# x's first mixer straight behind the first block, the context's choice beside it, and the context's gathered rows spread into layer 1

## The chip, the cores and the metric

One core of a Trainium2 chip runs the kernel. Its engines are PE (TensorE, matrix products), DVE (VectorE, element-wise work and reductions), ACT (ScalarE, activation functions and copies), POOL (GpSimd, here a queue that starts transfers) and SP (SyncE, the other queue that starts transfers). Each engine works through its own instructions in the order in which they stand. The metric is the device time of one execution in microseconds (us); a run of the kernel before takes 3798.77 us (median of three).

## The reference

Everything is float32 on 256 tokens of width 1024. A first block makes x: a banded attention layer, a latent attention layer and a norm. A second block has two layers over x and over a context of 256 tokens. Each layer makes from a conditioning vector the shifts, scales and gates that modulate both streams, runs a mixer (attention over x and context together, a pooling branch, a convolution branch, gates), and then a feed-forward with experts (PEER):

```python
xn = modulate(rms_norm(h, norm1_g[l]), mod[:, 0], mod[:, 1])
cn = modulate(rms_norm(hc, norm1_g[l]), mod_c[0], mod_c[1])
...                                   # q, k, v of x; k, v of the context
o = blocked_diff_attn(q, jnp.concatenate([k, kc], axis=1), jnp.concatenate([v, vc], axis=1), lam)
mix = mixer_output(o, p, ...)
if not last: hc = hc + mod_c[2] * mix_c          # the context's own mixer: layer 0 alone
h = h + mod[:, 2] * mix
h = h + mod[:, 5] * peer_ffn(xn2, ...)
if not last: hc = hc + mod_c[5] * peer_ffn(cn2, ...)   # the context's feed-forward: layer 0 alone
```

`peer_ffn` scores every token against two sets of 128 keys per head, takes the 16 best of each and the 16 best sums (the choice), and so picks 8 x 16 of 16384 experts per token. An expert is a row of `peer_u` (a dot product with the token, then gelu) and a row of `peer_v` (added with the gate as weight).

## The kernel before

Weights that are not read whole are split into a high part (ACT cast, L277, `wa`) and a rest (DVE subtraction, L278, `wb`), and a product is three matmuls (L405 to L407). For x the feed-forward is dense: `peer` walks the 16384 experts in 128 tiles of 128; `hid` makes a tile's activations, `wgt` multiplies them with a table of gates `G` that `gbuild` has written to memory (L1412), and `vside` (L1475 to L1477) adds the tile to four accumulators. For the context it is sparse: `rows` gathers 512 blocks (256 of `pu`, 256 of `pv`; block i holds the i-th chosen expert's row for each of 128 tokens, 512 KB) by an indirect transfer on POOL (L1335), and DVE makes a dot product (L1346) or a weighted addition (L1355) of each. Below, such a block is called a row.

The program is a set of Python generators. Each `yield` gives an estimate of the work just written, and combinators decide whose instructions come next: `par` advances the generator that is least far on relative to its total, `along` advances a side generator by a rate times the main one's cost, `chain` puts generators behind one another. A scheduling layer then rearranges a little within a window of some tens of instructions. So the order on each engine is fixed when the program is built.

`program` writes these stages in this order (L1569 to L1616), with the times of the profile below:

- 0 to 835 us: `b1`, the first block, beside the context's mixer of layer 0 and behind that the context's choice (`choose`, that is `topk` with `rows=True`); `mods` of layer 0 beside the context's attention.
- 835 to 1262: x's mixer of layer 0, with rows at a rate of 0.28 (`RATE[0]`).
- 1262 to 1575: `ffn_start` of layer 0: x's choice (`topk`), `gbuild`, the first tiles of `hid`, `mods` of layer 1 (48 blocks of `wmod`, 96 matmuls at L554 that the profile counts as 192), and rows at 0.28.
- 1575 to 2459: the tiles of `peer`, with rows by `par` and the total 270 (`RLEFT`); the rows that are left run on alone, and `rows_add` adds the context's sum.
- 2459 to 2911: x's mixer of layer 1; the context's norm, k and v (`kv_ctx`) beside x's q, k and v.
- 2911 to the end: `ffn_start` and `peer` of layer 1, without rows and without `mods`.

Tiles of one size share a pool of 42 buffers (`pg`).

Of the kernel before, what the change touches and what calls it, by code (L numbers as in the profile page):

```python
# [9 lines left out]
F32 = mybir.dt.float32  # L10
# [29 lines left out]
AT = 350.0  # L40
RLAG, RDEPTH = 20, 4
RATE, RLEFT = (0.28, 0.28), 270.0
# [246 lines left out]
class Ker:  # L289
# [228 lines left out]
    def mods(s, l, eng):  # L518
# [21 lines left out]
        for g in range(3):  # L540
            if g == 1 and l == 0:
                s.mod_scale(l, (("a1", "n1", 1),))
                yield None
                lim = 48
                for i in range(NMD):
                    load(16 + i)
            bank = s.ps("m")
            for q in range(16):
# [7 lines left out]
                if q % 4 == 3 and q < 15:  # L556
                    yield 2.0
# [578 lines left out]
    def mixer(s, l, st, src, ws, eng, res, kvx, late=None, before=None, seq=False, h=None, rbs=None):  # L1136
# [10 lines left out]
        qg = s.qkv(l, hn, ws, rope, True, r)  # L1147
        yield from (qg if before is None else par(s, (qg, 100.0), (before, 80.0)))
        o = Act(s, F32, "o")
        kv = [(r["k"], r["v"])] + kvx()  # L1150
        sr, q = r.pop("sr"), r.pop("q")
        if st == 1:
            for i in range(2):
                eng.dma_start(s.kvd[i], r["k"].t[i].rearrange("p k t -> p (k t)"))
                eng.dma_start(s.kvd[2 + i], r["v"][i])
        r.clear()
        more = [(late, 20.0)] if late is not None else []
        if seq:
            yield from par(s, (s.attn2(l, q, kv, sr, o), 60.0), *more)
            del q, kv, sr  # L1160
            yield from s.branches(l, hn, ws, r)
        else:
            yield from par(s, (s.attn2(l, q, kv, sr, o), 60.0), (s.branches(l, hn, ws, r), 190.0), *more)
            del q, kv, sr
# [142 lines left out]
    def rows(s, xn, out):  # L1307

        nc, v = s.nc, s.nc.vector
        xr = []  # L1310
# [226 lines left out]

def until(g):
# [18 lines left out]
def ffn_start(k, l, rx, ws, G, pe, tot, *more):  # L1557
# [5 lines left out]
    yield from par(k, (chain(tk, lambda: k.gbuild(rx, G, eng)), TG), (until(pe), tot), *more)  # L1563


def program(k, upto):
# [15 lines left out]
    def choose():  # L1582
        yield from k.topk(0, rc["xn"], wc, gp, rc, rows=True)
        cn.append(rc.pop("xn"))
    drain(par(k, (b1, 300.0),
              (chain(k.mixer(0, 1, ctx0, wc, gp, rc, lambda: [], md, seq=True, h=hc.pop(), rbs=rbc.pop()),
                     choose), AT),
              (k.setup2(), 100.0)))
    if upto < 3:
        return  # L1590
    rows = k.rows(cn, acc)
    ws = WS(k, ai["w2"][0], sy, whole=WHOLE)
    drain(along(k.mixer(0, 0, k.hd["x"], ws, sy, rx, lambda: [k.kv_load(sy)], seq=SEQ, h=x3.pop()), rows, RATE[0]))
    kp = {}
    pe = k.peer(0, rx["xn"], k.G[0], sy, sy, *NPRE[0], k.hd["x"], kp)
    drain(along(ffn_start(k, 0, rx, ws, k.G[0], pe, NPRE[0][1] * 3.41, (k.mods(1, gp), 60.0)), rows, RATE[1]))
    rx.clear()
    drain(par(k, (pe, 130 * 5.12), (rows, RLEFT)))
# [31 lines left out]
```

## Time and profile before

| | us |
|---|---|
| median of three runs (3797.86 to 3800.38) | 3798.77 |
| the profiled execution | 3794.38 |
| its span, first to last instruction | 3792.6 |
| PE busy | 3334.0 (88%) |
| DVE busy | 2739.1 (72%) |
| ACT busy | 1495.4 (39%) |
| POOL busy | 904.3 (24%) |

The profile is one execution on the chip. Busy is the time in which an engine ran an instruction; PEclk is the share of TensorE's full clock (2.4 GHz) that was granted; the DMA share is the mean busy share of the 16 transfer engines. Matmuls are pipelined, so one that lasts 0.28 us can be followed by the next after 0.12 us, and a busy PE is not at its peak. Waits are inferred from semaphores.

### The profile page before, as it was taken

The page shows a single profiled execution, that of the slowest core. Times are in us where ns is not written, and L with a number is a line of the kernel's source. Part 1 is how long each engine was busy: PE and PEld are TensorE (multiplying, and loading weights), DVE is VectorE, ACT ScalarE, POOL GpSimd, SP SyncE. Part 2 cuts the span into 40 slices and gives each one's busy share as a digit, 9 for nine tenths or more (in the row PEclk, how much of TensorE's full clock was granted, in tenths as well). Part 3 has the DMA queues.
Part 4 walks back from the last instruction along what each step waited for, and adds up shares of the span by engine and source line. Part 5 has one row for each costly group of instructions (what it writes and reads, how often), then busy time and mean ns, then how long its engine had stood idle before and what let it go on. Part 6 is the DMA issues. An engine that isn't in the chain of part 4 may idle for free.

```text
span 3792.6 us, 58009 instructions
## 1 busy us (share of the span) xinstructions
PE 3334.0 (88%) x21940; PEld 2974.1 (78%) x21940; DVE 2739.1 (72%) x5629; ACT 1495.4 (39%) x2807; POOL 904.3 (24%) x863
## 2 busy tenths in 40 slices
PE   7998999969899857789999994299999699999999
PEld 6966999857898844678888884187998588999998
DVE  4356775597898797898888899855765986555555
ACT  3444553213544122334444442142552154544444
POOL 2010011112223325655445457600000030000000
PEclk9988999978899879899999997598999899999999
DMA  8554445426678739999999999841445097666664
GB/s 295 178 182 136 133 147 186 179 84 255 217 249 312 283 138 398 403 401 372 363 370 370 371 369 361 331 156 58 154 150 200 23 289 256 216 211 210 211 210 143
DMA packets 249945, 907.32 MB, mean 239 GB/s; under 512 B 27632, under 2 KB 29712, under 8 KB 249664
## 3 DMA queue, kind: packets, MB, share of 16 engines
q1 hardware_dynamic: 126240, 454.09, 34.1%
q0 software_dynamic: 123424, 449.52, 32.6%
q8 instruction: 172, 2.82, 0.3%
q14 instruction: 109, 0.89, 0.1%
HBM read 861.53 MB, written 45.11 MB: 239 GB/s over the span
## 4 chain that ended last, share of the span: by engine, by line
PE 46%; DVE 7%; DMA 5%; issue 3%; ACT 1%; POOL 1%; DVEq 0%; ACTq 0%; POOLq 0%
PE pu L407 8%; PE pu L405 7%; PE pu L406 7%; PE pm L1475 5%; PE pm L1476 5%; PE pm L1477 5%; PE pu L412 3%; DMA row<-in_pu,ridx 2%; DMA row<-in_pv,ridx 1%; DVE wb L278 1%; DVE racc L1355 1%; PE pm L1403 1%; ACT wa L277 1%; DMA wm<-in_wmod 1%; POOL row L1335 1%
## 5 line engine op out<-in xcount | busy, mean ns | idle before, releaser
L278 DVE TENSOR_TENSOR wb<-wr,wa 128x1024 fp32r<-128x1024 f32 x846 | 1011.0, 1221 | 322.4 <-ACT wa L277 310.4
L277 ACT CAST wa<-wr 128x1024 fp32r<-128x1024 f32 x846 | 854.6, 1048 | 23.4 <-DMA wr<-in_w 17.8
L405 PE MATMUL pu<-hnh,wa 128*128 128x256 f32 x2000 | 584.4, 292 | 24.9 <-ACT wa L277 22.3
L407 PE MATMUL pu<-hnh,wb 128*128 128x256 f32 x2000 | 581.6, 291 | 8.2 <-DVE wb L278 8.2
L406 PE MATMUL pu<-hnl,wa 128*128 128x256 f32 x2000 | 580.6, 291 | 1.5 <-DVE hnl L501 1.3
L406 PE MATMUL pu<-xl,wa 128*128 128x256 f32 x1760 | 499.9, 284 | 9.2 <-DVE xl L1444 9.2
L405 PE MATMUL pu<-xh,wa 128*128 128x256 f32 x1760 | 499.7, 284 | 6.3 <-ACT xh L1443 3.9
L407 PE MATMUL pu<-xh,wb 128*128 128x256 f32 x1760 | 499.8, 284 | 0.8 <-DVE wb L278 0.8
L1335 POOL DMA_INDIRECT row<-in_pv,ridx x256 | 362.8, 1417 | 385.1 <-DVE wb L278 131.1
L1335 POOL DMA_INDIRECT row<-in_pu,ridx x256 | 332.3, 1298 | 472.4 <-PE pu L407 113.8
L405 PEld LDWEIGHTS pu<-hnh,wa 128*128 128x128 f32 x2000 | 398.3, 199 | 32.5 <-ACT wa L277 26.2
L1475 PE MATMUL pm<-wa,W 128*128 128x512 f32 x1024 | 368.2, 397 | 60.1 <-ACT wa L277 58.4
L1476 PE MATMUL pm<-wb,W 128*128 128x512 f32 x1024 | 409.8, 400 | 4.5 <-DVE wb L278 4.3
L407 PEld LDWEIGHTS pu<-hnh,wb 128*128 128x128 f32 x2000 | 397.2, 199 | 15.4 <-DVE wb L278 11.0
L1477 PE MATMUL pm<-wa,W 128*128 128x512 f32 x1024 | 404.2, 395 | 0.0
L406 PEld LDWEIGHTS pu<-hnl,wa 128*128 128x128 f32 x2000 | 398.4, 199 | 4.0 <-DVE hnl L501 2.5
L405 PEld LDWEIGHTS pu<-xh,wa 128*128 128x128 f32 x1760 | 339.1, 193 | 20.4 <-ACT wa L277 7.4
L406 PEld LDWEIGHTS pu<-xl,wa 128*128 128x128 f32 x1760 | 339.0, 193 | 16.5 <-DVE xl L1444 9.6
L407 PEld LDWEIGHTS pu<-xh,wb 128*128 128x128 f32 x1760 | 339.3, 193 | 2.3 <-DVE wb L278 1.0
L1346 DVE CUSTOM_DVE_ANT_0 row<-row,xr 128x1024 f32<-128x1024 f32 x256 | 310.9, 1219 | 28.0 <-DMA row<-in_pu,ridx 28.0
L1355 DVE SCALAR_TENSOR_TENSOR racc<-row,rwg,racc 128x1024 f32<-128x1024 f32 x254 | 325.4, 1281 | 7.5 <-DMA row<-in_pv,ridx 6.8
L412 PE MATMUL pu<-xn,wr 128*128 128x256 f32 x1344 | 320.7, 397 | 4.8 <-ACT xn L514 4.8
(403 smaller groups left out, 5408.7 us busy)
## 6 DMA issues: line engine op xcount, KB each, us to landing
wr<-in_w SPq DMA_DIRECT2D x288, 512.0 KB
wr<-in_pu SPq DMA_DIRECT2D x256, 512.0 KB
wr<-in_pv SPq DMA_DIRECT2D x256, 512.0 KB
wr<-in_w POOLq DMA_DIRECT2D x130, 512.0 KB
wm<-in_wmod POOLq DMA_DIRECT2D x96, 512.0 KB
G<-gt POOLq DMA_DIRECT2D x64, 512.0 KB
gp<-G SPq DMA_DIRECT2D x32, 512.0 KB
gp<-G POOLq DMA_DIRECT2D x32, 512.0 KB
```

The source lines that it names most:

```text
L277: nc.scalar.copy(a, r)
L278: nc.vector.tensor_tensor(b, r, a, op=OP.subtract)
L405: mm(out, ah, bh, start=i == 0, stop=False)
L406: mm(out, ah, bl, start=False, stop=False)
L407: mm(out, al, bh, start=False, stop=i == n - 1)
L412: s.nc.tensor.matmul(out, w[:, k * 128:(k + 1) * 128], x(k), start=k == 0, stop=k == 7)
L1335: nc.gpsimd.indirect_dma_start(out=t, out_offset=None, in_=tab[w], in_offset=bass.IndirectOffsetOnAxis(ap=s.ridx[:, tt, i:i + 1], axis=0))
L1346: v.tensor_tensor_reduce(t, t, xr[tt], 1.0, 0.0, OP.mult, OP.add, hid[:, i:i + 1])
L1355: v.scalar_tensor_tensor(out[tt], t, wg[:, i:i + 1], out[tt], op0=OP.mult, op1=OP.add)
L1475: mm(bank, wh, vh[:, c], start=j == 0, stop=False)
L1476: mm(bank, wh, vl[:, c], start=False, stop=False)
L1477: mm(bank, wl, vh[:, c], start=False, stop=j == 127)
```

## The change

What it does, part by part:

1. `b1` and x's mixer of layer 0 become one chain, and a new combinator `lead` follows it with side generators: the context's mixer and choice, then the rows, at twice the chain's cost (`RATE[0]` = 2.0); a row there has the cost 6.25, so rows come at 0.32 per unit. `rows` waits until the choice has been written.
2. `mods` of layer 1 moves from x's `ffn_start` of layer 0 to the context's choice, by `par` with 69 to 26. Its yields become finer. `mods` of layer 0 stands beside the context's branches, and not beside its attention.
3. Rows: 0.32 in x's mixer, 0.25 in `ffn_start`, 0.45 per unit beside the tiles of `peer` (a tile is 5.12), 0.3 beside x's q, k and v of layer 1, and the rest ahead of `rows_add` in `kv_ctx`. By the two instruction orders, rows stand in x's mixer, `ffn_start`, the tiles and behind the tiles thus: before 100, 53, 272, 87; now 113, 41, 300, 58.
4. In x's mixer of layer 1, `kv_ctx` stands no longer beside q, k and v: it is chained ahead of the attention, and that chain runs beside the branches.
5. `gbuild` starts the writes of `G` from ACT and not from POOL.

```diff
--- before.py
+++ after.py
@@ -37,9 +37,9 @@
 W1, NMD = 8, 5
 SEQ, TY = False, 1.0
 SW, ST = 40.0, 240.0
-AT = 350.0
 RLAG, RDEPTH = 20, 4
-RATE, RLEFT = (0.28, 0.28), 270.0
+RATE = 2.0, 0.32, 0.25, 0.45, 0.3, 2.0
+RLATE = 150.0
 GS = 2.0 ** 15
 DEPTH, LEAD = 3, 2
 DU, LU, DV, LV = 2, 1, 2, 1
@@ -544,6 +544,7 @@
                 lim = 48
                 for i in range(NMD):
                     load(16 + i)
+                yield 1.0
             bank = s.ps("m")
             for q in range(16):
                 kt, hf = q // 2, q % 2
@@ -553,8 +554,8 @@
                     j = hf * 2 + jj
                     nc.tensor.matmul(bank[32 * j:32 * j + 32, :], s.cs[:, kt, :],
                                      w[:, jj * 512:(jj + 1) * 512], start=kt == 0, stop=kt == 7)
-                if q % 4 == 3 and q < 15:
-                    yield 2.0
+                if q < 15:
+                    yield 0.5
             ev = s.s2([128, 512], "mev")
             nc.scalar.copy(ev, bank)
             tb = s.ps("m")
@@ -1133,7 +1134,8 @@
                 v.tensor_tensor(mrg.pair(i), mrg.pair(i), th, op=OP.add)
             yield 2.6
 
-    def mixer(s, l, st, src, ws, eng, res, kvx, late=None, before=None, seq=False, h=None, rbs=None):
+    def mixer(s, l, st, src, ws, eng, res, kvx, late=None, before=None, seq=False, h=None, rbs=None, side=None):
+
 
         nc, v = s.nc, s.nc.vector
         rope = st == 0
@@ -1144,24 +1146,33 @@
         del h, rbs
         yield 1.0
         r = {}
-        qg = s.qkv(l, hn, ws, rope, True, r)
-        yield from (qg if before is None else par(s, (qg, 100.0), (before, 80.0)))
-        o = Act(s, F32, "o")
-        kv = [(r["k"], r["v"])] + kvx()
-        sr, q = r.pop("sr"), r.pop("q")
+        yield from (s.qkv(l, hn, ws, rope, True, r) if side is None else
+                    along(s.qkv(l, hn, ws, rope, True, r), side, RATE[4]))
+        o = []
         if st == 1:
             for i in range(2):
                 eng.dma_start(s.kvd[i], r["k"].t[i].rearrange("p k t -> p (k t)"))
                 eng.dma_start(s.kvd[2 + i], r["v"][i])
+        q, sr, kv = r.pop("q"), r.pop("sr"), [(r["k"], r["v"])]
         r.clear()
+
+        def attend():
+            o.append(Act(s, F32, "o"))
+            kv.extend(kvx())
+            yield from s.attn2(l, q, kv, sr, o[0])
+            kv.clear()
         more = [(late, 20.0)] if late is not None else []
         if seq:
-            yield from par(s, (s.attn2(l, q, kv, sr, o), 60.0), *more)
-            del q, kv, sr
-            yield from s.branches(l, hn, ws, r)
+            yield from attend()
+            del q, sr
+            yield from par(s, (s.branches(l, hn, ws, r), 30.0), *more)
+        elif before is not None:
+            yield from par(s, (chain(before, attend), RLATE), (s.branches(l, hn, ws, r), 150.0), *more)
+            del q, sr
         else:
-            yield from par(s, (s.attn2(l, q, kv, sr, o), 60.0), (s.branches(l, hn, ws, r), 190.0), *more)
-            del q, kv, sr
+            yield from par(s, (attend(), 60.0), (s.branches(l, hn, ws, r), 190.0), *more)
+            del q, sr
+        o = o.pop()
         s.dump(f"o{l}{st}", o)
         mrg = r.pop("mrg")
         yield from s.gate_add(ws, hn, o, mrg)
@@ -1307,6 +1318,8 @@
     def rows(s, xn, out):
 
         nc, v = s.nc, s.nc.vector
+        while not xn:
+            yield 0.0
         xr = []
         cn = xn.pop()
         for tt in range(2):
@@ -1535,6 +1548,23 @@
         yield from g() if callable(g) else g
 
 
+def lead(main, *sides):
+
+    t, live = 0.0, [[g, r, 0.0] for g, r in sides]
+    for c in main:
+        t += c or 0.0
+        for e in live:
+            while e[2] < t * e[1]:
+                d = next(e[0], math.inf)
+                e[2] += d or 0.0
+        yield c
+
+
+def scaled(g, f):
+    for c in g:
+        yield c * f
+
+
 def until(g):
 
     for c in g:
@@ -1560,7 +1590,7 @@
     tk = k.topk(l, rx["xn"], ws, eng, rx)
     for i in range(SOLO):
         yield next(tk, None)
-    yield from par(k, (chain(tk, lambda: k.gbuild(rx, G, eng)), TG), (until(pe), tot), *more)
+    yield from par(k, (chain(tk, lambda: k.gbuild(rx, G, k.nc.scalar)), TG), (until(pe), tot), *more)
 
 
 def program(k, upto):
@@ -1582,32 +1612,31 @@
     def choose():
         yield from k.topk(0, rc["xn"], wc, gp, rc, rows=True)
         cn.append(rc.pop("xn"))
-    drain(par(k, (b1, 300.0),
-              (chain(k.mixer(0, 1, ctx0, wc, gp, rc, lambda: [], md, seq=True, h=hc.pop(), rbs=rbc.pop()),
-                     choose), AT),
-              (k.setup2(), 100.0)))
-    if upto < 3:
-        return
     rows = k.rows(cn, acc)
     ws = WS(k, ai["w2"][0], sy, whole=WHOLE)
-    drain(along(k.mixer(0, 0, k.hd["x"], ws, sy, rx, lambda: [k.kv_load(sy)], seq=SEQ, h=x3.pop()), rows, RATE[0]))
+    ctx = chain(k.mixer(0, 1, ctx0, wc, gp, rc, lambda: [], md, seq=True, h=hc.pop(), rbs=rbc.pop()),
+                lambda: par(k, (choose(), 69.0), (k.mods(1, gp), 26.0)))
+    xs = chain(b1, lambda: k.mixer(0, 0, k.hd["x"], ws, sy, rx, lambda: [k.kv_load(sy)], seq=SEQ, h=x3.pop()))
+    drain(lead(xs, (chain(ctx, lambda: scaled(rows, RATE[0] / RATE[1])), RATE[0]), (k.setup2(), 0.5)))
     kp = {}
     pe = k.peer(0, rx["xn"], k.G[0], sy, sy, *NPRE[0], k.hd["x"], kp)
-    drain(along(ffn_start(k, 0, rx, ws, k.G[0], pe, NPRE[0][1] * 3.41, (k.mods(1, gp), 60.0)), rows, RATE[1]))
+    drain(along(ffn_start(k, 0, rx, ws, k.G[0], pe, NPRE[0][1] * 3.41), rows, RATE[2]))
     rx.clear()
-    drain(par(k, (pe, 130 * 5.12), (rows, RLEFT)))
-    k.rows_add(0, acc, kp)
-    acc.clear()
+    drain(along(pe, rows, RATE[3]))
     if upto < 5:
         return
     ws = WS(k, ai["w2"][1], sy, whole=WHOLE)
     wc = WS(k, ai["w2"][1, 8:24], gp)
 
     def kv_ctx():
+        yield from scaled(rows, RATE[5])
+        k.rows_add(0, acc, kp)
+        acc.clear()
         hn = k.norm_hl(kp.pop(1), lambda i: k.a1[1][:, i, 1:2], k.mod(1, 1, 0), "hnc")
         yield 1.0
         yield from k.qkv(1, hn, wc, False, False, rc)
-    drain(k.mixer(1, 0, k.hd["x"], ws, sy, rx, lambda: [(rc.pop("k"), rc.pop("v"))], before=kv_ctx(), h=kp.pop(0)))
+    drain(k.mixer(1, 0, k.hd["x"], ws, sy, rx, lambda: [(rc.pop("k"), rc.pop("v"))], before=kv_ctx(), h=kp.pop(0),
+                  side=rows))
     pe = k.peer(1, rx["xn"], k.G[1], sy, gp, *NPRE[1], ao)
     drain(ffn_start(k, 1, rx, ws, k.G[1], pe, NPRE[1][1] * 3.41))
     rx.clear()
```

PE around the context's choice (L1207 and L412 before, L1218 and L412 now, `pm<-keyT` and `pu<-xn`). Before, the choice has PE to itself and x's norm (L471) follows:

```order
L1207 MATMUL pm_7803<-keyT_7468,qf_7801 128x128 x4
L412 MATMUL pu_7931<-xn_7393,wr_7842 128x256 x4
L412 MATMUL pu_7931<-xn_7394,wr_7842 128x256 x4
L412 MATMUL pu_7931<-xn_7393,wr_7883 128x256 x4
L412 MATMUL pu_7931<-xn_7394,wr_7883 128x256 x2
L1207 MATMUL pm_7854<-keyT_7468,qf_7852 128x128 x4
L412 MATMUL pu_7931<-xn_7394,wr_7883 128x256 x2
L1207 MATMUL pm_7903<-keyT_7468,qf_7901 128x128 x4
L1207 MATMUL pm_7950<-keyT_7468,qf_7948 128x128 x4
L471 MATMUL pm_8099<-ones,sq_8100 128x1 x8
L471 MATMUL pm_8099<-ones,sq_8110 128x1 x8
```

Now matmuls of the first block's last product (`ogh`, `ogl`) and of `mods` (L555, `wm`) stand between:

```order
L406 MATMUL pu_7774<-ogl_6464,wa_7678 128x256
L407 MATMUL pu_7774<-ogh_6462,wb_7679 128x256
L555 MATMUL pm_7570<-wm_7726,cs 32x512 x2
L1218 MATMUL pm_7648<-keyT_6918,qf_7646 128x128 x4
L412 MATMUL pu_7813<-xn_6822,wr_7636 128x256 x4
L412 MATMUL pu_7813<-xn_6823,wr_7636 128x256 x4
L412 MATMUL pu_7813<-xn_6822,wr_7716 128x256 x4
L412 MATMUL pu_7813<-xn_6823,wr_7716 128x256 x3
L1218 MATMUL pm_7746<-keyT_6918,qf_7744 128x128 x4
L412 MATMUL pu_7813<-xn_6823,wr_7716 128x256
L555 MATMUL pm_7570<-wm_7730,cs 32x512 x2
L405 MATMUL pu_7905<-ogh_6461,wa_7777 128x256
```

The choice's matmuls have moved into the first block's end, and `mods` of layer 1 with them.

POOL in `gbuild` of layer 0, before: gathers of rows (L1335), loads for `mods` (L536) and writes of `G` (L1412) in one queue:

```order
L536 DMA wm_13682<-in_wmod 128x1024
L536 DMA wm_13686<-in_wmod 128x1024
L536 DMA wm_13690<-in_wmod 128x1024
L536 DMA wm_13694<-in_wmod 128x1024
L1335 DMA row_13698<-in_pv,ridx 128x1024
L1412 DMA G_96<-gt_13477 128x8x128
L1412 DMA G_96<-gt_13478 128x8x128
L1412 DMA G_96<-gt_13479 128x8x128
```

ACT at the same place now: the writes of `G` (L1425) stand behind the evictions that fill them (`gt`), and POOL's queue there holds gathers alone:

```order
L1420 ACTIVATE gt_13483<-pm_13633 128x32x4
L1420 ACTIVATE gt_13484<-pm_13633 128x32x4
L1425 DMA G_96<-gt_13481 128x8x128
L1425 DMA G_96<-gt_13482 128x8x128
L1425 DMA G_96<-gt_13483 128x8x128
L1425 DMA G_96<-gt_13484 128x8x128
L1420 ACTIVATE gt_13653<-pm_13663 128x32x4
L1420 ACTIVATE gt_13654<-pm_13663 128x32x4
```

DVE behind the last tile of layer 0, before: rows, and between them only x's norm for layer 1 (L392, L474) at the very end:

```order
L1346 ISA row_22468,rhid<-row_22468,xr_8237 128x1024
L1346 ISA rhid 128x1
L1355 SCALAR_TENSOR_TENSOR racc_18006<-row_22471,rwg,racc_18006 128x1024
L1346 ISA row_22474,rhid<-row_22474,xr_8237 128x1024
L1346 ISA rhid 128x1
L1355 SCALAR_TENSOR_TENSOR racc_18006<-row_22477,rwg,racc_18006 128x1024
L474 TENSOR_REDUCE ss_22632<-pm_22611 128x2
L392 TENSOR_SCALAR rt_22636<-ss_22632 128x2
L1346 ISA row_22480,rhid<-row_22480,xr_8237 128x1024
```

DVE in x's q, k and v of layer 1 now: a row between every one or two weight rests (L278, `wb`):

```order
L278 TENSOR_TENSOR wb_22597<-wr_22561,wa_22596 128x1024
L1359 ISA row_22557,rhid<-row_22557,xr_8469 128x1024
L1359 ISA rhid 128x1
L278 TENSOR_TENSOR wb_22632<-wr_22594,wa_22631 128x1024
L1363 TENSOR_TENSOR rwg<-rwg,rgate 128x16
L1368 SCALAR_TENSOR_TENSOR racc_17674<-row_22591,rwg,racc_17674 128x1024
L278 TENSOR_TENSOR wb_22662<-wr_22629,wa_22661 128x1024
L1359 ISA row_22625,rhid<-row_22625,xr_8469 128x1024
L1359 ISA rhid 128x1
L278 TENSOR_TENSOR wb_22697<-wr_22659,wa_22696 128x1024
L278 TENSOR_TENSOR wb_22732<-wr_22694,wa_22731 128x1024
L1368 SCALAR_TENSOR_TENSOR racc_17674<-row_22690,rwg,racc_17674 128x1024
```

So 58 rows have moved past the start of x's mixer of layer 1, and none stands alone.

## Rows read from the trace of the kernel before

**Rows 1.** The page's slices: PE's busy share in tenths, 40 slices of 94.8 us.
```profile
PE   7998999969899857789999994299999699999999
```

**Rows 2.** Stages: stretch, length, busy us per engine (instructions), clock, DMA share, GB/s.
```profile
core 0: us, PE busy (x) PEld busy (x) DVE busy (x) ACT busy (x) POOL busy (x), PEclk, DMA share, GB/s
0.00:200.00 200.00, 177.38 (x1196) 162.70 (x1197) 86.77 (x154) 82.98 (x111) 29.94 (x59) 0.95 0.67 232
200.00:420.00 220.00, 196.12 (x1230) 147.86 (x1229) 146.86 (x472) 104.36 (x265) 20.72 (x39) 0.89 0.43 147
420.00:720.00 300.00, 291.46 (x2356) 285.49 (x2354) 188.29 (x392) 134.49 (x226) 43.87 (x83) 0.98 0.50 168
720.00:795.00 75.00, 67.85 (x323) 59.76 (x323) 53.17 (x306) 9.90 (x18) 3.18 (x6) 0.91 0.31 115
795.00:835.00 40.00, 11.21 (x51) 10.83 (x51) 39.86 (x233) 3.25 (x7) 0.00 (x0) 0.54 0.05 14
835.00:945.00 110.00, 100.78 (x625) 88.40 (x626) 81.30 (x124) 39.84 (x52) 39.41 (x31) 0.87 0.74 273
945.00:1262.00 317.00, 291.57 (x2138) 272.73 (x2136) 269.82 (x473) 141.49 (x228) 105.14 (x85) 0.93 0.74 259
1262.00:1390.00 128.00, 88.20 (x441) 73.16 (x441) 110.08 (x542) 15.16 (x36) 20.18 (x29) 0.81 0.54 205
1390.00:1540.00 150.00, 121.32 (x851) 79.18 (x849) 117.66 (x190) 53.83 (x274) 82.78 (x88) 0.89 0.90 345
1540.00:1575.00 35.00, 21.09 (x131) 19.64 (x130) 23.30 (x30) 10.40 (x17) 20.91 (x19) 0.80 1.02 406
1575.00:1700.00 125.00, 106.40 (x507) 87.67 (x508) 120.11 (x167) 45.15 (x73) 71.36 (x54) 0.92 1.02 403
1700.00:2314.00 614.00, 570.83 (x3574) 512.63 (x3573) 541.35 (x713) 259.13 (x404) 306.92 (x213) 0.99 0.97 369
2314.00:2459.00 145.00, 22.94 (x113) 20.14 (x112) 132.75 (x201) 14.21 (x24) 108.24 (x85) 0.54 0.94 354
2475.00:2630.00 155.00, 149.78 (x923) 133.39 (x925) 70.10 (x100) 54.11 (x67) 4.78 (x9) 0.91 0.36 119
2630.00:2850.00 220.00, 212.85 (x1668) 202.25 (x1667) 156.75 (x292) 113.57 (x195) 0.00 (x0) 0.97 0.44 143
2850.00:2911.00 61.00, 57.17 (x466) 55.67 (x465) 34.71 (x68) 21.97 (x27) 1.06 (x2) 0.98 0.44 153
2911.00:3023.00 112.00, 83.37 (x393) 72.11 (x391) 87.64 (x508) 14.43 (x32) 0.00 (x0) 0.85 0.24 90
3023.00:3118.00 95.00, 88.94 (x769) 79.42 (x769) 82.08 (x132) 54.42 (x278) 24.72 (x28) 0.96 0.80 250
3118.00:3148.00 30.00, 27.94 (x216) 27.61 (x217) 13.73 (x17) 14.31 (x26) 4.64 (x6) 0.94 0.85 314
```

**Rows 3.** PE's waits, 720 to 835: total us, times, longest.
```profile
PE pm L482 <- DVE dg L479: 22.9, 1, 22.9
```

**Rows 4.** Line L554, 36 to 51: count, duration ns, first and last start.
```profile
L554 PE MATMUL pm<-wm,cs x64: 592/592/617, 36.6 to 47.4; 128*32 128x512 f32 x64
```

**Rows 5.** Groups by line, 1390 to 1540: count, busy us, mean ns, idle before.
```profile
L554 PE MATMUL pm<-wm,cs 128*32 128x512 f32 x140 | 35.6, 690 | 14.2 <-DMA wm<-in_wmod 14.1
...
L1412 POOL DMA_DIRECT2D G<-gt x29 | 26.6, 921 | 65.2 <-ACT gt L1407 58.2 <-DMA G<-gt 2.2 <-DMA row<-in_pv,ridx 2.1
```

**Rows 6.** DVE groups, 2314 to 2459.
```profile
L1355 DVE SCALAR_TENSOR_TENSOR racc<-row,rwg,racc 128x1024 f32<-128x1024 f32 x56 | 72.0, 1286 | 5.0 <-DMA row<-in_pv,ridx 4.7
L1346 DVE CUSTOM_DVE_ANT_0 row<-row,xr 128x1024 f32<-128x1024 f32 x36 | 44.2, 1227 | 4.2 <-DMA row<-in_pu,ridx 4.2
```

**Rows 7.** Waits of DVE and PE among the tiles, 1750 to 2250.
```profile
DVE gel L1457 <- ACT gel L1434: 42.8, 20, 3.3
...
PE pm L1475 <- ACT wa L277: 34.6, 20, 2.0
```

**Rows 8.** Line L730, SP's transfers with four pieces per partition: duration ns min/median/max.
```profile
L730 SPq DMA_DIRECT2D bias<-bias_rows x4: 359/378/458, 195.8 to 202.7; - x4
```

## The prediction

> **What bounds the kernel now.** I read the page's slices first, then one table of busy times cut at the stages' ends, then the waits at the places that it singles out. In the slices [rows 1] PE, the busiest engine, is near full nearly everywhere and falls to 2 and 4 tenths in two slices at about 2300 to 2450 us. The stage table [rows 2] says what stands there: from 2314 to 2459 PE is busy 23 of 145 us, while DVE is busy 133 and the transfers are at 0.94. These are the context's rows that the tiles left over, 56 and 36 of them [rows 6]; layer 1 waits for nothing but its turn behind them in DVE's queue. The second hole is the context's choice, 720 to 835: PE is busy 79 of 115 us, and its longest wait, 22.9 us, is for DVE, which still sorts [rows 2, 3]. The third is x's own choice and the gates, 1262 to 1575: 231 of 313 us, DVE 251 [rows 2]. Elsewhere PE decides. x's mixer of layer 1 (2475 to 2911) has PE busy 420 of 436 us; the same mixer of layer 0, with rows beside it (835 to 1262), 392 of 427, with DVE at 351 [rows 2].
>
> **The change part by part.** I add the steps to the profiled execution (3794.4 us, of which the span is 3792.6); the median of the runs is 4.4 us longer, and the sum is carried over to it as it is.
>
> *To the start of x's first mixer.* The work of 0 to 720 stays. The choice brings the 68 us that PE was busy with it in 720 to 795. `mods` brings 192 matmuls; 64 of them alone took 11.1 us from the first start to the end of the last [rows 4], so 0.173 each and 33 us. Behind the first block's last product come its norm and x's norm, with little to cover them: 10 us for the tail of a stage, as from 3783 to the end of the span at 3792.6, and 16 us for a norm, as between the ends of two stretches, 2459 and 2475 [rows 2]. 720 + 68 + 33 + 26 = 847 in place of 835: +12. The cover for the choice's 93 us of DVE is the first block's second attention, which has DVE work of its own. Ends: -15, if the new order fills half of the 55 us that PE stood idle before 720, busy 665 [rows 2]; +58, if half of those 93 us stand in series with the attention. I take the sum, near the lower end, since DVE is busy only 422 of those 720 us. The loads of `mods` go into POOL's queue among the weights' loads; transfers are at a third to two thirds there, so I price that at nothing; where loads were short, in 1390 to 1540, PE waited 14 us for them [rows 5], which is that price if the cover fails.
>
> *x's mixer of layer 0.* 13 rows more, at 1.25 us of DVE (116 us for 92) [rows 6]: 16 us on an engine that is busy 351 of 427. A third of it shows: +5, ends 0 and +16.
>
> *Choice, gates, first tiles.* Without rows and `mods`, layer 1 does this in 112 + 95 + 30 = 237 us, with DVE busy 183 [rows 2]. Now 41 rows stand in it, 51 us of DVE. If 10 of them hide in the gap before the first tile (DVE busy 14 of 30), it takes 278, where it took 128 + 150 + 35 = 313: -35. Ends: -51, if half the rows hide; -18, if the rows' transfers hold it up as now. The writes of `G` leave POOL, where 29 of them took 27 us and waited 58 for `gt`, with gathers queued behind [rows 5]; that loosening is in the 278.
>
> The Trainium skill (DMA: Bandwidth & Descriptors, Issuing engines are not separate DMA queues) holds that another issuing engine only saves the sequencer's issue time. By that this part would be worth at most those 27 us of POOL, which is not the bound; the wait in the same row is what the rule leaves out.
>
> On ACT the 32 writes per layer cost between 0.38 us each, SP's transfers with four pieces a partition [rows 8], and 0.92, POOL's for the same write [rows 5]: 12 to 29 us, on an engine busy 54 of 95 us in the gates of layer 1 [rows 2]. +3, ends 0 and +28.
>
> *The tiles of layer 0.* 300 rows in place of 272. In 1700 to 2314 PE ran 3574 matmuls, 36 a tile, so 99 tiles at 6.2 us. In each four tiles DVE waits once, 2.1 us, for PE's next tile, and PE once, 1.7, for ACT, 20 waits each in 500 us [rows 7]; 0.9 row more per four tiles is 1.1 us of DVE, less than the wait in front of it. The early tiles, 1575 to 1700, have DVE at 96% and transfers at 403 GB/s: the 5 rows more there show in full, 524 KB at 403 each, 6 us. Ends: +6, and +40 if all 28 show at the 369 GB/s of the later tiles. I take +14, a quarter of the remaining difference, because the early tiles show that 403 can be had and the later ones would need 369 x 18.2/17.3 = 388 (17.3 blocks per four tiles: 8 weights, 1 of gates, 8.3 rows).
>
> The skill's page DMA: Bandwidth & Descriptors (Where 436 GB/s comes from) puts what the memory gives one core at about 358 GB/s. By that the tiles are at the limit already and the end is +40; the 403 [rows 2] is against it, in this trace.
>
> *Layer 1's mixer.* Before, 2314 to 2911 is 597 us. Now the norm follows the last tile (10 us, as above). If the rows hid entirely, the rest would be 16 for the norm, 110 for q, k and v of x beside 28 rows (835 to 945 had 29 and took 110), 49 for k and v of the context (150 us PE busy in 2475 to 2630, less 101 in 835 to 945), 220 and 61 as now: 456. Two things come on top. Up to the last row DVE has 45 for q, k and v (81 less 29 x 1.25), 9 for the norm, 73 for the 58 rows and some 50, a third of 157, for the branches' first part: 177, at the 85% that it reached in 945 to 1262 208 us; PE has 16 + 101 + 73 there (a third of 220): 190. I take +16. And the attention now starts behind rows and `kv_ctx`, so its 16 steps crowd into the last third: in 200 to 420, where two attentions meet, PE was busy 196 of 220 [rows 2], so 24 lost; +23. 456 + 39 + 10 = 505: -92. Ends: -131 with both extras at nothing; -59 with both at nearly twice.
>
> Sum: 12 + 5 - 35 + 3 + 14 - 92 = -93. 3798.8 - 93 = 3706.
>
> **The rivals.**
>
> *Rows are free in layer 1 (R1).* Its PE is busy 420 of 436 us without rows, and DVE only 262: room for 73 us. Against it: layer 0's mixer with rows ran PE at a granted clock of 0.87 to 0.93, against 0.91 to 0.98 without. Then -131 in place of -92: 3667.
>
> *The rows come back as load (R2).* The tiles pay +40 and the late attention loses another 30. For: DVE at 88 to 96% among the tiles, and transfers at 0.97. Against: the waits of 2.1 us. 3706 + 26 + 30 = 3762.
>
> *The hole only moves (R3).* The change would not do what it says: PE reaches `rows_add` in its queue, finds DVE still at rows, and idles there as it did from 2314. For: `rows_add` and `kv_ctx` stand ahead of the attention on PE. Against: some 73 us of branches stand ahead of them. All of the -92 is lost: 3798.
>
> *The choice holds up the first block (R4).* On DVE the choice's 93 us stand in front of the first block's second attention, whose every step needs DVE, and x's whole path waits for that block; before, the choice held up nothing but itself. In series it adds 93, and with the tiles at +40: 3706 + 93 + 26 = 3825. It makes the kernel slower from the point where x's first mixer starts later than 847 + 93 = 940. Against: PE has 124 us of work there that doesn't wait for that attention (68, 33, and the block's last product, 192 matmuls at 0.12), more than DVE's 93.
>
> **How the numbers follow.** The forecast 0.52 (with its own range 3675 to 3737), R1 0.18, R2 0.15, R3 0.07, R4 0.08. Changes under 0.2%, 7.6 us, are about what a measurement of this kernel cannot tell from none. Faster: the forecast, R1 and R2, 0.85; within 0.2%: R3, 0.07; slower: R4, 0.08. The range 3645 to 3775 leaves out R3, R4 and a little of R1's lower end. The single ends add up to far more on both sides, but they are separate places and do not fall together.
>
> **What would show it.** In the new profile: no slice with PE under 5 tenths behind the tiles of layer 0; x's first q matmul at about 847 (R4: past 940); `ffn_start` of layer 0 some 278 us long with no `wm` waits; tiles at 6.2 to 6.4 us (R2: 6.5); layer 1's mixer about 495 us from norm to norm, with DVE near 85% up to the last row. A PE wait of tens of us at `rows_add` would be R3. The forecast is wrong if the hole behind the tiles has closed and the time has not fallen by 50 us or more.

## The result, and the profile after

The changed kernel takes 3751.4 us (median of four runs, 3747.7 to 3753.4) against 3798.4: ratio 0.988, 95% interval 0.9866 to 0.9890. That is 47 us gained where 93 were forecast. The profiled execution has a span of 3748.1 us, 44.5 less than before.

PE's slices of the page after, to be held against [rows 1]:

```profile
PE   7989989997899876789999998878989689999999
```

The 4 and 2 behind the tiles (slices 25 and 26 of 40) are gone; two 8s, a 7 and an 8 stand there. The 6 of the context's choice (slice 9) is a 9 now, but a 7 follows it. The first eight slices have not got fuller.

Stage table after, columns as in [rows 2]:

```profile
0.00:690.00 690.00, 629.28 (x4415) 562.09 (x4416) 393.79 (x905) 299.31 (x546) 96.60 (x185) 0.93 0.52 182
690.00:878.00 188.00, 161.54 (x940) 118.29 (x938) 124.20 (x670) 36.64 (x84) 33.86 (x58) 0.91 0.59 219
878.00:1291.00 413.00, 380.15 (x2728) 351.30 (x2728) 360.30 (x596) 181.25 (x281) 169.93 (x116) 0.93 0.76 270
1291.00:1573.00 282.00, 192.41 (x1251) 167.53 (x1250) 236.79 (x742) 75.81 (x320) 58.21 (x48) 0.82 0.68 232
1573.00:1700.00 127.00, 103.83 (x465) 83.87 (x466) 122.18 (x169) 43.17 (x67) 77.11 (x56) 0.88 1.00 394
1700.00:2331.00 631.00, 586.09 (x3644) 525.96 (x3643) 580.71 (x768) 264.03 (x413) 348.05 (x235) 0.99 0.99 385
2331.00:2549.00 218.00, 181.62 (x1205) 166.95 (x1204) 175.62 (x280) 74.64 (x102) 68.80 (x53) 0.86 0.72 258
2549.00:2855.00 306.00, 276.02 (x2001) 256.90 (x2000) 185.73 (x364) 132.50 (x216) 8.97 (x17) 0.93 0.39 128
2855.00:2967.00 112.00, 82.87 (x390) 72.04 (x391) 88.21 (x509) 14.47 (x33) 0.00 (x0) 0.85 0.20 79
2967.00:3068.00 101.00, 92.40 (x768) 81.44 (x767) 78.31 (x126) 50.16 (x262) 0.00 (x0) 0.94 0.75 224
```

x's first mixer starts at 878, not at 847. Behind the tiles PE now works through what stood still from 2314 to 2459, but from 2331 to 2549, where the rows are, it is busy 182 of 218 us.

For all runs the span is cut at the same six events of the trace: the first q product of x's first mixer, the last product of the mixer, which stands behind `gate_add` and reads `mh` (mixer 0 ends; 9 us before the cut at 1262 in [rows 2]), the first tile's and the last tile's product, the same `mh` product in layer 1, and the first tile of layer 1. "Choice" stands for choice, gates and the lead-in of the tiles; "rows" are the row instructions on DVE behind the last tile. The tiles of layer 1 take 645 us in every run.

| run | median | x starts | mixer 0 | choice 0 | tiles 0 | mixer 1 | choice 1 | rows |
|---|---|---|---|---|---|---|---|---|
| before | 3798 | 835 | 417 | 322 | 745 | 583 | 245 | 88 |
| after | 3751 | 878 | 413 | 282 | 758 | 514 | 258 | 58 |
| forecast of the difference | -93 | +12 | +5 | -35 | +14 | -92 | +3 | |
| measured difference | -45 | +43 | -5 | -40 | +13 | -69 | +13 | |
| e1_g_from_pool | 3741 | 883 | 413 | 280 | 764 | 510 | 244 | 59 |
| e2_mods_by_attention | 3756 | 869 | 412 | 282 | 759 | 513 | 259 | 59 |
| e3_mods1_back | 3793 | 871 | 422 | 343 | 755 | 494 | 257 | 46 |
| e4_positions_early | 3758 | 878 | 413 | 285 | 757 | 515 | 255 | 58 |
| e5_rows_in_tiles | 3768 | 884 | 421 | 285 | 809 | 465 | 259 | 0 |
| e6_rows_spread_alone | 3774 | 857 | 414 | 321 | 749 | 539 | 248 | 89 |
| e7_lead_alone | 3796 | 881 | 417 | 287 | 758 | 545 | 258 | 58 |
| e8_choice_slower | 3762 | 710 | 569 | 285 | 753 | 540 | 257 | 82 |
| e9_mods1_back_pool | 3755 | 869 | 429 | 313 | 761 | 495 | 248 | 46 |
| e10_mods1_alone | 3799 | 859 | 414 | 293 | 751 | 590 | 245 | 95 |
| e11_no_lead | 3726 | 859 | 412 | 284 | 760 | 514 | 244 | 59 |
| e12_pool_more_rows | 3743 | 881 | 427 | 280 | 765 | 489 | 245 | 39 |

Stages are of one profiled execution each. The kernel before, run with e1 to e4, e5 to e8 and e9 to e12, had medians of 3796.0, 3794.7 and 3797.5 (13 runs each, 3788 to 3802). Up to the tiles e5's code is that of the changed kernel, and it comes to the first tile at 1590 where that had 1573 (6, 9 and 3 us in three stages; in the second the granted clock is 0.91 against 0.93), so a few us in one stage of two single profiles decide nothing. All four runs of e5 take 3766 to 3769, so a difference of this size between two totals need not be the edit's either: the experiments are read by the stage that their edit touches.

### The profile page after: what moved, and what is told of

Read it like the earlier page. It is cut to its first block, busy times and chain, and to the rows that moved or that the text cites. A ratio compares the mean times of both kernels' runs of the same rounds, so it can differ in the third digit from the quotient of the medians.

```text
span 3748.1 us, 57989 instructions
## 1 busy us (share of the span) xinstructions
PE 3352.2 (89%) x21940; PEld 2988.5 (80%) x21940; DVE 2734.6 (73%) x5629; ACT 1493.1 (40%) x2807; POOL 878.4 (23%) x799
## 3 DMA queue, kind: packets, MB, share of 16 engines
q10 hardware_dynamic: 66560, 33.56, 3.1%
## 4 chain that ended last, share of the span: by engine, by line
PE 45%; DVE 7%; DMA 3%; issue 2%; ACT 2%; ACTq 1%; POOL 0%; DVEq 0%; POOLq 0%
PE pu L405 7%; PE pu L407 7%; PE pu L406 7%; PE pm L1488 5%; PE pm L1489 5%; PE pm L1490 5%; PE pu L412 2%; DMA row<-in_pv,ridx 1%; DVE wb L278 1%; ACT wa L277 1%; DVE racc L1368 1%; ACTq L1425 1%; DMA G<-gt 1%; ACT gt L1420 1%; DVE row L1359 1%
## 5 line engine op out<-in xcount | busy, mean ns | idle before, releaser
L278 DVE TENSOR_TENSOR wb<-wr,wa 128x1024 fp32r<-128x1024 f32 x846 | 1013.2, 1223 | 328.1 <-ACT wa L277 312.8
L1348 POOL DMA_INDIRECT row<-in_pu,ridx x256 | 361.9, 1414 | 508.0 <-DVE wb L278 127.6
L1348 POOL DMA_INDIRECT row<-in_pv,ridx x256 | 366.1, 1430 | 487.5 <-DVE wb L278 100.7
L412 PE MATMUL pu<-xn,wr 128*128 128x256 f32 x1344 | 324.6, 398 | 4.8 <-ACT xn L514 4.8
L1447 ACT ACTIVATE gel<-pu 128x256 f32<-128x256 f32 x208 | 79.7, 383 | 602.7 <-PE pu L407 602.6
```

The costliest lines, as they stand in the source:

```text
L278: nc.vector.tensor_tensor(b, r, a, op=OP.subtract)
L412: s.nc.tensor.matmul(out, w[:, k * 128:(k + 1) * 128], x(k), start=k == 0, stop=k == 7)
L1348: nc.gpsimd.indirect_dma_start(out=t, out_offset=None, in_=tab[w], in_offset=bass.IndirectOffsetOnAxis(ap=s.ridx[:, tt, i:i + 1], axis=0))
L1447: nc.scalar.activation(g, bank[:, :NT], AF.Gelu_apprx_tanh)
```

## The experiments

**The writes of G (e1).** The changed kernel with one word put back:

```diff
-... lambda: k.gbuild(rx, G, k.nc.scalar)), TG), ...
+... lambda: k.gbuild(rx, G, eng)), TG), ...
```

> The changed kernel with the writes of G started from POOL again, in both layers. Theory (the writes on ACT cost layer 1 its 13 us): the stretch from x's choice of layer 1 to the first tile (2855 to 3103, 248 us with the change, 235 before) falls back to about 236, layer 0's (1304 to 1573) stays at 269 or grows by up to 5, since gathers queue behind the writes again; in total 8 to 13 us faster than the changed kernel. Rival (the 13 us are not the writes': another start of the stage): both stretches stay within 3 us, total within 4 us. Rival 2 (the gathers gain more than ACT loses): layer 0's stretch grows by 10 or more and the total is slower.

3741.0 us, ratio to before 0.9856 (0.9836 to 0.9876). Layer 1's choice and gates fall from 258 to 244, what they had before; layer 0's stay (280 against 282). In the table every kernel with these writes on POOL has 244 to 248 there, and every one with them on ACT 255 to 259. The gates of layer 1, 2967 to 3103 in the changed kernel: its waits (total us, times, longest), then its writes (duration ns min/median/max, first and last start), then the writes of e1:

```profile
ACT gt L1420 <- PE pm L1416: 14.2, 6, 3.8
...
PE pm L1416 <- ACT gt L1420: 7.5, 4, 3.0
...
ACT gt L1420 <- DMA G<-gt: 6.3, 1, 6.3
ACT gpre L1447 <- DMA G<-gt: 6.0, 1, 6.0
```

```profile
L1425 ACTq DMA_DIRECT2D G<-gt x32: 366/762/4003, 2979.0 to 3075.1; - x32
```

```profile
L1425 POOL DMA_DIRECT2D G<-gt x32: 885/885/913, 2983.9 to 3067.4; - x32
```

A write costs its issuer about as much on either engine, 0.76 and 0.89 us. On POOL, which does little else in this stage, the 32 go out within 84 us; on ACT, within 96, they stand in the line of the copies `gt` that empty PE's banks, one of them for 4 us, and PE waits 7.5 us for these copies.

**The modulation of layer 1 among the gates again (e3), and that with the writes from POOL (e9).** Both are the changed kernel with

```diff
-                lambda: par(k, (choose(), 69.0), (k.mods(1, gp), 26.0)))
+                choose)
...
-... NPRE[0][1] * 3.41), rows, RATE[2]))
+... NPRE[0][1] * 3.41, (k.mods(1, gp), 60.0)), rows, RATE[2]))
```

> The changed kernel with mods of layer 1 back in x's choice and gates of layer 0. Prediction's step (33 us of PE moved into the context's choice, and layer 0's stretch of choice and gates 35 us shorter for it and for 12 rows fewer): x's first mixer starts 30 to 38 us earlier (840 to 848), the stretch from 1304 to 1573 grows from 269 to about 285 to 300; total 5 us faster to 10 slower. Rival A3 (mods is what holds up the choice's tail): the start moves by 45 us or more and the total falls by 10 or more. Rival (mods is free in the choice, covered by DVE's sorting): the start moves by under 15 us, and the total grows by 15 or more.

> The changed kernel with the modulation of layer 1 back beside the gates of layer 0 and the writes of G from POOL again. With the modulation back and the writes on ACT, choice and gates of layer 0 took 343 us in place of 282. Theory A, ACT's queue is the reason (writes of G, which wait for gt, and the modulation's evictions stand in one line): with the writes on POOL the stage falls to about 322 as in the kernel before, layer 1 saves its 13 us: some 34 us under that run, about 3760. Theory B, the modulation itself costs that much among the gates whoever writes: only the 13 us of layer 1 come back, about 3780.

e3 takes 3793.0 (ratio 0.9996, 0.9984 to 1.0008): all the gain is gone, far past what was expected. Its x starts at 871, 7 us earlier than in the changed kernel and not 30 to 38, so by its figures the last rival came true: with x's chain beside it, the modulation is nearly free in the choice. e9, one word further, takes 3754.7 (0.9887, 0.9871 to 0.9904). The stage from mixer 0 to the tiles is 343 us in e3 and 313 in e9. ACT's waits among the gates and then the writes, 1425 to 1600 in e3, and the same, 1430 to 1580, in e9 (`mev` is the copy of a modulation product out of its bank):

```profile
ACT gt L1420 <- PE pm L1416: 33.7, 17, 4.8
ACT gt L1420 <- DMA wm<-in_wmod: 30.6, 2, 16.8
```

```profile
L1425 ACTq DMA_DIRECT2D G<-gt x31: 366/1350/10950, 1439.9 to 1599.0; - x31
```

```profile
ACT gt L1420 <- PE pm L1416: 37.4, 21, 5.5
...
ACT mev L560 <- PE pm L555: 22.9, 3, 15.2
```

```profile
L1425 POOL DMA_DIRECT2D G<-gt x28: 885/904/949, 1445.7 to 1563.4; - x28
```

Theory A of e9 holds: with its writes on ACT, the engine stood 30.6 us for the loads of `wm` and a write took up to 11 us; with the writes on POOL neither is there. The move of the modulation is worth 42 us only because the writes went to ACT, and 12 to 14 (3754.7 against 3741.0, ratios 0.9887 and 0.9856) without that. Why ACT came to stand for the loads of `wm` the profile does not show.

**The modulation of layer 1 beside the choice, alone (e10).** The kernel before with the two lines of e3's diff changed the other way and nothing else.

> The kernel before with one edit: the modulation of layer 1 runs beside the context's choice (par 69 to 26, as in the change) and no longer beside the gates of layer 0. Theory A, the move by itself fills the choice's 36 us of idle PE: x's first mixer starts within 12 us of 835, choice and gates of layer 0 get 40 to 50 us shorter, some 10 rows more are left over (1.4 us each): 20 to 30 us gained, about 3770. Theory B, it needs x's chain beside the choice: the 33 us of PE are paid at the choice, and what the gates give back goes to rows: 3785 or more.

3799.4 us, ratio 1.0009 (1.0000 to 1.0019): theory B. Its trace, first up to 720, then the choice:

```profile
0.00:720.00 720.00, 665.22 (x4774) 594.40 (x4774) 421.55 (x1017) 321.66 (x601) 93.65 (x180) 0.94 0.51 176
720.00:859.00 139.00, 111.75 (x581) 76.64 (x581) 98.10 (x558) 15.23 (x29) 36.92 (x63) 0.86 0.75 292
```

The 33 us of PE work are there (111.8 busy where 720 to 835 had 79.1 [rows 2]), but the idle time only falls from 36 to 27: x starts 24 us later. The gates give 30 back, and the shorter stage leaves 7 rows more in the hole behind the tiles.

**The spread of the rows alone (e6), and the first part alone (e7).** e6 is the kernel before with the new `mixer` and

```diff
-    drain(par(k, (pe, 130 * 5.12), (rows, RLEFT)))
-    k.rows_add(0, acc, kp)
-    acc.clear()
+    drain(along(pe, rows, 0.405))
...
     def kv_ctx():
+        yield from scaled(rows, RATE[5])
+        k.rows_add(0, acc, kp)
+        acc.clear()
```

e7 is the changed kernel with the opposite: `drain(rows)` and `rows_add` behind the tiles, and `kv_ctx` beside q, k and v as before.

> The kernel before with one part of the change alone: the rows that the tiles leave over (88) are not drained behind the tiles but run in layer 1, beside q, k and v and then in front of rows_add and kv_ctx in the chain with the attention. Nothing else moves. Theory A, a row costs layer 1 about 1.7 us of PE's time (the 12 rows fewer in the run with the modulation back in the gates shortened the mixer by 20 us): the mixer, 525 us with 58 rows, takes 576 with 88, against 597 before: 21 us gained, about 3775. Theory B, the spread hides most rows whatever their number: the whole difference of 69 us between the mixers, about 3727.

> The changed kernel with layer 1 as before: the rows left over run by themselves behind the tiles, then rows_add, and k and v of the context beside q, k and v of x. What is left of the change is the first part, x's mixer beside the context's choice, with the modulation in the choice and the writes of G on ACT. Theory A: the first part moves the time by its own sums, +43 at the start of x's mixer, -5, -40 in the choice and gates, +13 in the tiles, +13 in the gates of layer 1, and by 30 rows fewer behind the tiles at 1.37 us each, -41: -17 in all, about 3779. Theory B: the first part alone brings nothing or costs, the whole gain lies in layer 1: 3796 or more.

e6: 3774.3 (0.9945, 0.9928 to 0.9962). e7: 3795.5 (1.0006, 0.9996 to 1.0015). So the changes ahead of layer 1's mixer, the writes on ACT with them, bring nothing together. e6's mixer of layer 1 is 44 us shorter with as many rows as before, more than the 21 expected; the rest was lost ahead of x's start, at 857 in place of 835. With the new `mixer` e6 also runs the modulation of layer 0 beside the context's branches, not its attention. In 200 to 420 PE is busy 182.3 us there, against 196.1 [rows 2], and its longest wait is a new one, for a weight's first copy:

```profile
PE pu L406 <- ACT wa L278: 7.3, 1, 7.3
```

That the whole 22 us come from this move is not shown by it.

**That move undone (e2), and the positions' load moved (e4).** e2 is the changed kernel with the modulation of layer 0 beside the attention (`par(s, (attend(), 60.0), *more)`); e4 loads `posi` at the program's start.

> The changed kernel with mods of layer 0 back beside the context's attention, where it stood before. Theory A1 (x's first mixer starts at 878 and not at 847 because the context's attention, 196 to 290, has lost the matmuls that filled PE there; its clock was granted at 0.70 to 0.79 in 240 to 320): the start moves to 862 to 868, the total falls by 10 to 16 us. Rival A2 (POOL's queue: loads of weights wait behind one small load): start and total within 4 us of the changed kernel. Rival A3 (the choice's own tail, 830 to 878): within 4 us as well.

> The changed kernel with the small load of the positions (on POOL, L772) moved to the program's start, into a buffer that is free until the choice. Theory A2 (that load waits 26 us, 435 to 461, for a small buffer in POOL's queue, and the context's weights queue behind it, so that PE is busy only 67 of 80 us in 440 to 520): x's first mixer starts 8 to 14 us earlier, the total falls by 8 to 14. Rivals A1 and A3: under 4 us.

e2 is inconclusive, e4 a miss. e2's x starts at 869, 9 to 15 us earlier than in the five runs that share the changed kernel's start (878 to 884), but its four times are 3741 to 3761, median 3756.0 (0.9896, 0.9879 to 0.9913), and the profiled one is the fastest of them. e4, 3758.3 (0.9904, 0.9886 to 0.9923), starts x at 878: `posi` costs nothing there.

**The pace of the choice (e8).** The changed kernel with `RATE[0]` 1.5.

> The changed kernel with RATE[0] 1.5 in place of 2.0: the context's mixer and its choice advance at three quarters of the pace beside x's chain, so that more of the choice's vector work stands behind the first block and its norm in place of ahead of them. Theory A, the choice on DVE is what makes x's first mixer start at 878 and not at 847: the start comes at 855 or earlier. Theory B, the start is set by PE's own work and the first block's chain: it stays within 8 us of 878. In both the rows start later, so that the total may rise by up to 1.3 us for each row that is left for layer 1.

x's first q product comes at 710, 168 us earlier, which is theory A by its figure, but mixer 0 ends only 12 us earlier, at 1278. The two stages of e8, then of the changed kernel:

```profile
0.00:710.00 710.00, 637.20 (x4588) 575.13 (x4588) 415.04 (x1015) 317.97 (x600) 85.97 (x165) 0.92 0.51 176
710.00:1278.00 568.00, 518.26 (x3490) 448.53 (x3490) 436.61 (x1116) 197.61 (x307) 170.21 (x170) 0.93 0.70 249
```

```profile
0.00:878.00 878.00, 790.82 (x5354) 680.38 (x5354) 517.98 (x1573) 335.94 (x629) 130.46 (x243) 0.92 0.54 190
```

Up to the end of mixer 0 PE is idle 72.8 + 49.7 = 123 us in e8, 87.2 + 32.9 = 120 in the changed kernel (with the row of 878 to 1291 above), and 122 before, with 33 us less work (91 up to 835 [rows 2], 31 up to 1253). So a slower pace of the lead moves the idle time and does not remove it. The order as a whole does change it: without the lead the same work leaves 81.4 + 33.3 = 115 (e11), and with the lead but without the modulation in the choice it is 115.7 + 39.1 = 155:

```profile
0.00:871.00 871.00, 755.29 (x5150) 675.05 (x5150) 527.44 (x1575) 336.07 (x630) 114.03 (x201) 0.90 0.48 168
871.00:1293.00 422.00, 382.86 (x2725) 353.50 (x2726) 356.34 (x584) 180.40 (x277) 147.68 (x115) 0.92 0.74 263
```

Both lines are e3's. The 24 rows more that e8 leaves over then cost 26 us in mixer 1: 3762.2 (0.9922, 0.9902 to 0.9941).

**All rows among the tiles (e5), more rows beside mixer 0 (e12).** `RATE[3]` 0.545; and `RATE[1]` 0.38 with the writes from POOL.

> The changed kernel with RATE[3] 0.545 in place of 0.45, so that all rows left (58 in the changed kernel) run among the tiles of layer 0 and none in layer 1. Theory A, the rows' vector work is what layer 1's mixer pays for: the mixer falls from 525 us to about 466 (456 plus the 10 of the norm behind the last tile), 59 us, and the tiles pay what the last 31 rows cost them, 13 us for 31, so 24 us: 35 us under the changed kernel, about 3716. Theory B, the tiles are at the limit of the transfers (0.99 busy, 385 GB/s): each row is 524 KB, 1.36 us, so the tiles pay 79 us and the sum is 20 us over the changed kernel, about 3771.

> The changed kernel with the writes of G from POOL and RATE[1] 0.38 in place of 0.32: some 20 rows more beside x's mixer of layer 0, so as many fewer in layer 1. Theory A, rows are nearly free there (98 and 111 rows left it at 306 us from the first product with the cached keys to the end): layer 1 saves 0.85 us a row, 17 us, about 3725. Theory B, VectorE is full there (276 of 302 us busy): each row costs its 1.25 us, and the time stays at 3741 to 3750.

e5: 3768.1 (0.9927, 0.9910 to 0.9943). Tiles and mixer of layer 1 in e5:

```profile
1590.00:2399.00 809.00, 713.16 (x4109) 628.23 (x4110) 774.43 (x1015) 309.11 (x482) 472.25 (x341) 0.93 1.00 396
2399.00:2864.00 465.00, 439.22 (x3169) 409.80 (x3167) 288.62 (x541) 204.92 (x312) 9.57 (x18) 0.93 0.42 140
```

The 58 rows cost the tiles 51 us and save the mixer 49: 0.88 and 0.84 us each. The tiles pay between the two theories' 24 and 79. What one stage gains the other loses; of the 19 us between the two profiled spans 17 stand at the first tile already, where the kernels do not differ. e12: 3742.6 (ratio 0.9859, 0.9842 to 0.9875), no different from e1: 20 rows more lengthen mixer 0 by 14 us and shorten mixer 1 by 22, and the median shows nothing of the rest.

**Without x's chain beside the choice (e11).** The kernel before with e10's edit, e6's layer 1, the modulation of layer 0 beside the attention, the writes from POOL, and the changed kernel's rates 0.32, 0.25, 0.45 and 0.3 (the 0.28 in what was expected stands in its list of rates, but no line uses it).

> The kernel before with the modulation of layer 1 beside the context's choice and the rows spread into layer 1 (rates 0.32, 0.28, 0.45 and 0.3), but without x's chain beside the choice, with the modulation of layer 0 beside the attention as before and the writes of G from POOL. If these two parts carry the gain (theory A): 20 to 30 us by the first, 21 us by the spread plus some 18 that its own run lost ahead of x's mixer to the move of the modulation of layer 0: about 3730, under the changed kernel. If x's chain beside the choice is what makes room (theory B): 3750 or more.

3726.3 us (3720.4 to 3731.2), ratio 0.9818 (0.9802 to 0.9835): 25 under the changed kernel, 23 by the two ratios, and the fastest of all. Its start, to be held against the changed kernel's 878 us above (790.82 busy, clock 0.92), its mixer 0, and its layer 1:

```profile
0.00:859.00 859.00, 777.62 (x5354) 673.40 (x5354) 519.54 (x1573) 336.48 (x629) 130.56 (x243) 0.93 0.55 194
859.00:1271.00 412.00, 378.72 (x2722) 349.64 (x2723) 360.22 (x596) 181.50 (x281) 152.33 (x116) 0.93 0.76 273
...
2316.00:2829.00 513.00, 452.21 (x3162) 419.18 (x3160) 356.32 (x621) 204.81 (x314) 77.64 (x70) 0.90 0.51 181
2829.00:3074.00 245.00, 204.93 (x1417) 183.74 (x1416) 186.87 (x673) 84.03 (x332) 29.29 (x34) 0.90 0.55 185
```

Theory A holds: the same 5354 matmuls are done 19 us earlier without the lead, and everything behind that is as in e1. Of the 19, 6 are idle time (81 against 87) and 13 busy time, at a granted clock of 0.93 against 0.92. Ahead of that point e11 differs from the changed kernel in two more things, the place of layer 0's modulation (9 us by e2's profile) and the modulation's coarser yields, so the lead alone is not measured to the us.

## Why the prediction was right, and where it was not

The measured 3751 lies within 3645 to 3775, but outside the forecast's own 3675 to 3737, and nearer to R2's 3762 than to 3706. By the sign that the prediction gives itself, a closed hole and a time that has not fallen by 50 us, the forecast was wrong: the hole has closed and the time fell by 47 (42 to 51 by the interval). So the places of the gain were seen rightly, and its size was not.

**Start of x's first mixer, forecast +12, measured +43.** Two steps were in this sum. The modulation's 33 us hold as PE's work (e10), but what they cost depends on what stands beside them: 24 us without x's chain (835 to 859, e10), 7 with it (871 in e3, 878). The step that failed is the other, that x's chain beside the choice covers the choice's DVE work and that "the work of 0 to 720 stays". By the sum x should have started at 847 - 33 = 814 without the modulation, and came at 871 (e3); with it, 847 became 878, and without the lead it is 859 (e11). Ends from -15 to +58 held it. Of the 31 us that the start was off, 17 are idle time and 14 busy time: 847 left 70 us beside the 777 of PE's work, the changed kernel has 87 beside 791. The choice's 36 us of idle PE did close (27 idle in 690 to 878, with the tail of the first block in it), but 61 are idle up to 690, against 55 up to 720 for more work; and the same matmuls took 791 us at a granted clock of 0.92, where e11 has 778 at 0.93. The sum had the move of layer 0's modulation at nothing. e2, with that in its old place, stands between the two:

```profile
0.00:869.00 869.00, 783.63 (x5354) 675.70 (x5354) 518.54 (x1573) 336.36 (x629) 130.35 (x243) 0.93 0.54 192
```

So e2 puts 9 to 15 of the 31 to that move, by one profile; the rest was not taken apart between the lead and the modulation's finer yields. The first block's last product (`ogh`) ended at 595 before and ends at 834 now: x's chain stands beside the choice because it is held back. The mechanism of R4 was there in small: x's chain paid for the choice, though not its 93 us in series; 940 was never near. R4's 124 us of PE's work count the block's last product (23 us), which reads what the block's second attention writes (`og`), so 101 stood against the 93.

**Choice and gates of layer 0, forecast -35, measured -40.** Right in size. The modulation's leaving is 30 of it (e10); the rest is not taken apart. One reason given was wrong: the writes leaving POOL loosened nothing in this stage (282 against 280 in e1).

**Tiles, forecast +14, measured +13.** Right, and so is the reading that DVE's waits and the transfers had a little room: 31 rows cost 0.42 us each. e5 shows the end of it, transfers at 1.00 and 0.88 us a row. R2's 40 us were not paid.

**Layer 1's mixer, forecast -92, measured -69.** The hole closed as foreseen, and no wait of tens of us stands at `rows_add` (the longest of PE in 2331 to 2550 is 7.6 us, for a weight's first copy), which ends R3:

```profile
PE pu L405 <- ACT wa L277: 16.9, 3, 7.6
```

Rows were mis-sized: they were to cost 16 us there, and cost 49 (514 against 465 in e5). In the prediction's cut, 10 us later, e5's mixer is 475, where 456 + 10 + 23 = 489 stood for it without rows: norm and late attention cost some 14 us less than forecast, which hid a part of the rows' error. PE's matmuls are the same, its idle time is 61 us with rows and 26 without, and its busy time 13 us longer (452.6 against 439.2 in e5, clock 0.90 against 0.93):

```profile
2331.00:2845.00 514.00, 452.57 (x3167) 419.23 (x3166) 356.29 (x621) 205.50 (x315) 77.77 (x70) 0.90 0.52 180
```

R1, rows for nothing, falls. R2 was right in part: the rows did come back as load, but in the mixer (33 us over their price) and not in the tiles.

**The writes on ACT, forecast +3, measured +13.** The ends, 0 to 28, held it; e1 gives it back. In [rows 5] the 58 us of POOL's waiting for `gt` had looked like a price of the old place; it was idle time of an engine that was not the bound.

The errors, +31, -10 (mixer 0), -5, -1, +23 and +10, are the 48 us between -93 and -45. The gain is thus layer 1's mixer (-69), the choice's stage (-40) and mixer 0 (-5), less what x's chain and the modulation pay at the start (+43), the tiles (+13) and the writes (+13).

The Trainium skill (DMA: Bandwidth & Descriptors, Issuing engines are not separate DMA queues) says that another issuing engine saves only the sequencer's time. By that rule this part would have gained at most POOL's 27 us of issuing; e1 shows no gain in layer 0 and 13 us lost in layer 1, on the engine that took the writes over. The Trainium skill (the same page, Where 436 GB/s comes from) gives about 358 GB/s from memory for a core, as half of what two cores share. One core runs here, and e5's tiles moved 396 for 809 us, so in this case the measurement stands against that figure as a limit.

## What to carry to other kernels

Work that fills a hole beside a dependent chain is worth what PE's idle time up to the next common point loses, not the hole's length: add the idle time of all stages up to that point before and after, as e8 and e10 show, and the busy time with it, since the same matmuls took 778 and 791 us in two orders. Rows of vector work are not free because their engine has room on average; price them by running a stage with and without them. A DMA moved to another engine is paid in that engine's line, so look at what is queued behind it there, and test the parts of a change one by one: here the lead, with the modulation's move that came along with it, and the writes on ACT cost some 25 us together, and the version without them was the fastest.

## What the runs showed of the hardware

The same 33.6 MB of `G` leave ACT in 66,560 packets of about 504 B, and take 3.1% of the 16 engines' span. The queues of the changed kernel's page:

```profile
q0 software_dynamic: 114208, 415.96, 30.5%
q10 hardware_dynamic: 66560, 33.56, 3.1%
```

From POOL they are part of this row of e1's page, 9,216 packets more than the row above, so about 3.6 KB each and 2.8% of the span:

```profile
q0 software_dynamic: 123424, 449.52, 33.3%
```
